# A one-layer encoder kernel: tile offsets of 512 bytes, and another order of its first loads

## The chip, the core and the metric

The kernel runs on one core of a Trainium2 chip. The core has a matrix engine, TensorE (PE; its weight loads are shown apart, as PEld), three engines for elementwise work, VectorE (DVE), ScalarE (ACT) and GpSimd (POOL), and SyncE (SP), which here issues most of the DMAs. A tile lies in SBUF, 128 partitions of one and the same byte offset each; matmul results go to PSUM, in banks of 128x512 floats. The metric is the device time of one execution in microseconds (us), the median of several runs.

## What is computed

One residual layer on x of 1024 tokens by 1024 channels, in float32: a norm; one projection into pooling channels and q, k, v; a pooling mixer; differential attention with 8 heads; two gated branches; an output projection; then a norm and a squared-ReLU MLP of width 4096. Cut to what matters:

```python
h = rmsnorm(x, g_mix[l])
z = h @ w_in[l]
...
y_pool = pool_mixer(u_pool, w_pool_grp[l], pool_scale[l])
y_attn = diff_attention(q, k, v, g_q[l], g_k[l], lam, g_sub[l], lambda_init)
gates = jax.nn.sigmoid(h @ w_gate[l] + b_gate[l])
merged = (gates[..., :D_MODEL] * (y_pool @ w_branch_pool[l])
          + gates[..., D_MODEL:] * (y_attn @ w_branch_attn[l]))
x = x + merged @ w_out[l]
h2 = rmsnorm(x, g_ffn[l])
x = x + jnp.square(jax.nn.relu(h2 @ w_up[l])) @ w_down[l]
```

The rmsnorm is `x * rsqrt(mean(x*x) + EPS) * g`, with g a row of 1024 numbers that every token uses.

## The kernel before

**Products.** Every float32 operand is split in two parts of a reduced format, hi and lo (`split`, L117: a cast on ACT, then a subtraction on DVE or POOL, L119 and L120). A product is three matmuls, hi by hi, hi by lo, lo by hi (`mm3`, L125 to L127). In `nc.tensor.matmul(ps, a, b)` a is the weights (128x128, loaded anew for every matmul) and b the columns that stream past them (128x512 for most groups, 128x384 for z, 128x256 for po).

**Stages.** In order of time: norm and projection z per head and token tile, with attention (scores sc, transposed maps ta, output po) interleaved, and in the gaps the gate projection g and the pooling projection u; then bp (pool branch), ba (attention branch), op (output projection), and the MLP. The MLP multiplies by a scheme of seven block products instead of eight: X, Y, Z, W for the up projection (16 pairs), and Da, Db for the down projection (56 steps of 24 matmuls). A planner orders the instructions of each engine by priority and dependence; `issue_after` holds back a block of instructions on one engine until a given one of that engine has been issued.

**Places in SBUF.** Tiles are taken from pools, and pools lie one behind the other in the order in which they are opened: const (identf, mhalf, ones, inv, cols, gs, zero, and two buffers each of nss and nrs), hp0 and hp1 (hT, later mT and others), wpool (split weights: wqkv, fwgate, wba, wo), rpool, fp (fr, and two buffers of fo, 528 floats each), fq, up (U tiles: K, V, maps, yT, raw inputs), and, during attention, sp, which holds small tiles (ss, rs, rows, ms, nm, cf) and larger ones (dist, qn, Q, oqs) mixed. Each tile takes a multiple of 32 bytes per partition. The MLP's pools replace these; some grow from the left again (BT tiles, A and AS operands, and w in the last stage), those with side="right" from the top of SBUF downwards (B11 and B21, the raw weights, and u in the last stage).

**The start.** START (L43) lists the first steps. `x0` loads the first token tile in two halves (L322); `g` loads the row g into all 128 partitions of gmb (L368); `n0` norms token tile 0 (`norm_transpose`, halves=True: one half's sum of squares on ACT at L268, the other's on DVE at L269, the power on POOL at L274), multiplies x by rs and g (L280), transposes on TensorE (L285) and splits into hT; `w0` to `w3` load the weights of the first head, two issues each (L332); `s` steps split them. All these loads go through SP's queue, in that order. Then follow the small loads rows, gqk and lqk (L373 to L381). The first z product needs hT of tile 0 and the split weights.

```python
START = "x0 g n0 w0 w1 w2u w3u x1 s0p s1 x2 s2p s3 x3"
...
gmb = ut([P, D], F32, "gmb")
nc.sync.dma_start(gmb, g_mix[0].partition_broadcast(P))
...
nc.vector.scalar_tensor_tensor(hn[:, js], xt[:, js], rs, gb[:, js], op0=ALU.mult, op1=ALU.mult)
```

Of the kernel before, what the change touches and what calls it, by code (L numbers as in the profile page):

```python
# [17 lines left out]
P = 128  # L18
S = 1024
# [22 lines left out]

START = "x0 g n0 w0 w1 w2u w3u x1 s0p s1 x2 s2p s3 x3"  # L43
NX = [-2, -1, 0, 0, 0, 1, 2, 3]
# [13 lines left out]
def encoder_kernel(  # L58
# [26 lines left out]

    const = ctx.enter_context(tc.tile_pool(name="const", bufs=1))
    dram = ctx.enter_context(tc.tile_pool(name="dram", bufs=1, space=DRAM))
    mix = ctx.enter_context(ExitStack())
# [25 lines left out]
    def f(ap):  # L114
        return ap.bitcast(F32)
# [25 lines left out]
    def fo_tile(name):  # L141
        return fp.tile([P, 528], F32, tag="fo", name=name, bufs=N_FO)

# [92 lines left out]

    identf = const.tile([P, P], F32, name="identf")
    make_identity(nc, identf)
    mhalf = const.tile([P, NT], F32, name="mhalf")
    nc.gpsimd.memset(mhalf, -0.5)  # L240
    ones = const.tile([P, P], F32R, name="ones")
    nc.gpsimd.memset(f(ones), 1.0)
# [3 lines left out]

    cols = const.tile([P, 32], F32, name="cols")
    gs = const.tile([P, 1], F32, name="gs")
# [12 lines left out]
    def norm_transpose(xt, gb, t, dst, hn, small, banks, halves=False):  # L261
# [16 lines left out]
        for j in range(2):  # L278
            js = slice(j * 512, (j + 1) * 512)
            nc.vector.scalar_tensor_tensor(hn[:, js], xt[:, js], rs, gb[:, js], op0=ALU.mult, op1=ALU.mult)  # L280
            trp, trtag = banks[j % len(banks)]
            ps = trp.tile([P, 512], F32, tag=trtag, name=f"hps{t}_{j}")
            for i in range(4):
                k = 4 * j + i
                nc.tensor.transpose(ps[:, i * P : (i + 1) * P], hn[:, k * P : (k + 1) * P], identf)  # L285
# [12 lines left out]

    with ExitStack() as ph:
        sp = ph.enter_context(tc.tile_pool(name="sp", bufs=1))  # L300
        ps_s = ph.enter_context(tc.tile_pool(name="ps_s", bufs=N_S, space=PSUM))
# [3 lines left out]
        def s1(shape, dt, name, tag, bufs=1):  # L305
            return sp.tile(shape, dt, tag=tag, name=name, bufs=bufs)

        xs = {}

# [8 lines left out]
        def load_x(t):  # L318
            xs[t] = ut([P, D], F32, f"x{t}")
            for c in range(0, D, 512 if t == 0 else D):  # L320
                e = c + 512 if t == 0 else D
                nc.sync.dma_start(xs[t][:, c:e], x[t * P : (t + 1) * P, c:e])  # L322

# [4 lines left out]

        def load_w(h, kp, raw_fn=raw):
            rw = raw_fn([P, 2, 384], f"rqkv{h}_{kp}")  # L330
            for i in range(2):
                nc.sync.dma_start(  # L332
                    rw[:, i, :].rearrange("p (s c) -> p s c", s=3),
                    w_qkv[:, 2 * kp + i, :, h * P : (h + 1) * P],
                )
            raws[h, kp] = rw

        def norm_x(t):
            if t % 4 == 0:
                hT.update(alloc_T(htile, "hT", t // 4))  # L340
            if FU >> t & 1:
                hn = fu_tile(f"hn{t}")
            else:
                hn = ut([P, D], F32, f"hn{t}")
            banks = [(ps_t, "tr"), (ps_s, "sc")][: 2 if t < N_SC else 1]
            norm_transpose(xs.pop(t), gmb, t, hT, hn, sp, banks, t == 0)

# [9 lines left out]
        for w in START.split():  # L357
            if w[0] == "x":
                load_x(int(w[1]))
            elif w[0] == "n":  # L360
                norm_x(int(w[1]))
            elif w[0] == "w":
                load_w(0, int(w[1]), utf if w[2:] else raw)
            elif w[0] == "s":
                split_w(0, int(w[1]), nc.gpsimd if w[2:] else nc.vector)
            elif w[0] == "g":
                gmb = ut([P, D], F32, "gmb")
                nc.sync.dma_start(gmb, g_mix[0].partition_broadcast(P))  # L368


        rows = sp.tile([32, P], F32, name="rows")
        nc.gpsimd.memset(rows, 0.0)
        nc.sync.dma_start(rows[0:16, :], b_gate[0].rearrange("(r p) -> r p", p=P))  # L373
# [18 lines left out]
        def columns():  # L392
            cols_ps = ps_t.tile([P, 512], F32, tag="tr", name="cols_ps")
            nc.tensor.transpose(cols_ps[:, 0:32], rows, identf[0:32, 0:32])
            nc.vector.tensor_copy(cols, cols_ps[:, 0:32])
            nc.vector.tensor_scalar(gs, cols[:, 20:21], 1.0 - LAMBDA_INIT, None, op0=ALU.mult)
# [66 lines left out]
        def stage_qkT(h, t):  # L463
# [302 lines left out]
    gate_units = gates()  # L766
    for _ in range(G_FIRST):
        next(gate_units)
# [563 lines left out]
```

## Time and profile before

| | |
|---|---|
| median of 3 runs | 1557.21 us (1557.16 to 1557.71) |
| the profiled execution | 1556.93 us, its span 1555.1 us |
| first matmul | 8.89 us after the span's start |
| matmuls | 7649, of which 553 are transposes |
| stages by start of their matmuls | z from 10.9, bp 702.4 to 746, ba 746.0 to 836, op 836 to 928, MLP up 929 to 1243, MLP down from 1243.5 |
| mean DMA rate | 133 GB/s |

The profile is one execution, taken on the chip. A row of the timeline gives start and duration in us, the engine, the line, the operation, the tiles (written <- read) and, in brackets, how long the engine had been idle and what ended that. A group's row gives the same for all instructions of a kind, with their count and either the busy time and the mean ns of one, or minimum, median and maximum in ns. A window's row gives, for a stretch of the span, the busy time of an engine and its count of instructions, then the granted clock, the share of the DMA engines and GB/s. Ends of matmuls are modelled, so a matmul of 0.39 us can be followed by another 0.23 us after its start; what counts is the distance from start to start.

### The profile page before, as it was taken

The numbers are of one execution on the slowest core, as the hardware profiler recorded it, in microseconds if no ns is written. First come the engines' busy times: TensorE is split into PE (matmuls) and PEld (weight loads), VectorE is DVE, ScalarE is ACT, GpSimd is POOL, SyncE is SP. The second block draws the span as 40 slices with busy tenths as digits, with TensorE's granted clock in tenths as the row PEclk, the third lists the DMA queues.
The fourth block names the chain that finished last, engine by engine and source line by source line (L and its number), as shares of the span: only waits on it lengthen the run. The fifth ranks groups of instructions, "written<-read, shape, count | busy, mean of one in ns | idle before, by whom it ended". The sixth has DMA issues, their size and how long they took to land.

```text
span 1555.1 us, 22054 instructions
## 1 busy us (share of the span) xinstructions
PE 1535.1 (99%) x7649; PEld 1321.5 (85%) x7649; DVE 1012.4 (65%) x2268; ACT 816.0 (52%) x1808; POOL 350.2 (23%) x447
## 2 busy tenths in 40 slices
PE   7999999999999999999999999999999999999999
PEld 6999999999998989888888887888888788888887
DVE  6777677777878787765322448766665668556662
ACT  6656556656566556566432456565555634333331
POOL 5433334243425262324453400000000000000000
PEclk9999999999999999999999999999999999999999
DMA  7111212021202031547426524554432789537750
GB/s 229 47 56 48 65 41 68 24 74 40 72 28 84 28 96 42 176 151 235 143 92 198 178 102 122 179 183 159 136 135 109 273 312 385 179 122 256 224 189 27
DMA packets 166681, 206.41 MB, mean 133 GB/s; under 512 B 10069, under 2 KB 102954, under 8 KB 166570
## 3 DMA queue, kind: packets, MB, share of 16 engines
q1 hardware_dynamic: 149162, 177.71, 35.3%
q10 hardware_dynamic: 17408, 27.30, 4.7%
q8 instruction: 60, 0.98, 0.3%
q14 instruction: 51, 0.42, 0.1%
HBM read 150.42 MB, written 54.56 MB: 132 GB/s over the span
## 4 chain that ended last, share of the span: by engine, by line
PE 89%; DVE 4%; issue 2%; DMA 2%; ACT 2%; POOL 1%; POOLq 0%; SPq 0%; ACTq 0%; DVEq 0%
PE z L125 5%; PE z L127 5%; PE z L126 5%; PE Da L126 4%; PE Da L125 4%; PE Da L127 4%; PE g L125 3%; PE g L126 3%; PE g L127 3%; PE Db L126 3%; PE Db L125 3%; PE Db L127 3%; PE X L125 2%; PE X L126 2%; PE X L127 2%; PE sc L509 2%
## 5 line engine op out<-in xcount | busy, mean ns | idle before, releaser
L125 PE MATMUL z<-wqkv,hT 128*128 128x384 f32 x512 | 174.9, 342 | 0.5 <-DVE qn L451 0.3
L127 PE MATMUL z<-wqkv,hT 128*128 128x384 f32 x512 | 174.7, 341 | 0.5 <-DVE hT L120 0.4
L126 PE MATMUL z<-wqkv,hT 128*128 128x384 f32 x512 | 174.0, 340 | 0.0
L520 ACT ACTIVATE s<-s,nm 128x256 f32<-128x256 f32 (+7 forms) x128 | 99.6, 778 | 45.4 <-DVE nm L512 40.7
L259 POOL TENSOR_TENSOR ms<-ms,mhalf 128x4 f32<-128x4 f32 x64 | 66.5, 1040 | 159.0 <-DVE ms L258 140.6
L126 PE MATMUL g<-hT,fwgate 128*128 128x512 f32 x256 | 101.1, 395 | 0.0
L125 PE MATMUL g<-hT,fwgate 128*128 128x512 f32 x256 | 101.0, 394 | 0.1
L127 PE MATMUL g<-hT,fwgate 128*128 128x512 f32 x256 | 101.0, 395 | 0.0
L125 PEld LDWEIGHTS z<-wqkv,hT 128*128 128x128 f32 x512 | 97.1, 190 | 4.3 <-DVE qn L451 1.0
L127 PEld LDWEIGHTS z<-wqkv,hT 128*128 128x128 f32 x512 | 96.9, 189 | 3.1 <-DVE hT L120 1.2
L126 PEld LDWEIGHTS z<-wqkv,hT 128*128 128x128 f32 x512 | 97.1, 190 | 2.9
L512 DVE CUSTOM_DVE_ANT_0 s<-sc,dist 128x512 f32<-128x512 f32 (+3 forms) x128 | 74.6, 586 | 19.5 <-PE sc L510 18.1
L120 POOL TENSOR_TENSOR wqkv<-rqkv,wqkv 128x384 fp32r<-128x384 f32 x60 | 63.7, 1078 | 19.8 <-ACT wqkv L119 19.8
L120 DVE TENSOR_TENSOR AS<-s,AS 128x512 fp32r<-128x512 f32 x64 | 43.9, 688 | 36.1 <-ACT AS L119 35.9
L509 PE MATMUL sc<-K,Q 128*128 128x512 f32 (+2 forms) x192 | 66.8, 354 | 0.1
L510 PE MATMUL sc<-K,Q 128*128 128x512 f32 (+2 forms) x192 | 66.4, 354 | 0.0
L457 POOL TENSOR_TENSOR qn<-qn,ggh 128x128 f32<-128x128 f32 x64 | 32.3, 505 | 138.7 <-DVE qn L451 127.6
L483 ACT CAST Q<-tk 64x128 fp32r<-64x128 f32 x128 | 33.2, 259 | 57.9 <-DVE Q L482 56.0
L480 ACT CAST Q<-tk 64x128 fp32r<-64x128 f32 x128 | 33.0, 258 | 53.5 <-DVE K L479 52.1
L120 POOL TENSOR_TENSOR fwgate<-frgate,fwgate 128x512 fp32r<-128x512 f32 x32 | 43.9, 1376 | 52.3 <-ACT fwgate L119 52.1
L127 PEld LDWEIGHTS g<-hT,fwgate 128*128 128x128 f32 x256 | 48.1, 188 | 8.7
L125 PEld LDWEIGHTS g<-hT,fwgate 128*128 128x128 f32 x256 | 48.2, 188 | 7.4 <-ACT go L755 0.4
(429 smaller groups left out, 4647.0 us busy)
## 6 DMA issues: line engine op xcount, KB each, us to landing
wd<-in_w_down_dram SPq DMA_DIRECT2D x56, 512.0 KB, 5.3
wu<-in_w_up_dram SPq DMA_DIRECT2D x32, 512.0 KB, 5.0
udS<-us SPq DMA_DIRECT2D x64, 256.0 KB, 2.2
ur<-udS SPq DMA_DIRECT2D x32, 512.0 KB, 3.5
rqkv<-in_w_in_dram SPq DMA_DIRECT2D x64, 192.0 KB, 2.8
ud<-u ACTq DMA_DIRECT2D x48, 256.0 KB, 2.9
ur<-ud SPq DMA_DIRECT2D x24, 512.0 KB, 4.9
frgate<-in_w_gate_dram SPq DMA_DIRECT2D x32, 256.0 KB, 2.8
```

The source lines that it names most:

```text
L120: (lo_eng or nc.vector).tensor_tensor(lo, src, f(hi), op=ALU.subtract)
L125: nc.tensor.matmul(ps, lhs_hi, rhs_hi, start=first, stop=False, **kw)
L126: nc.tensor.matmul(ps, lhs_hi, rhs_lo, start=False, stop=False, **kw)
L127: nc.tensor.matmul(ps, lhs_lo, rhs_hi, start=False, stop=last, **kw)
L259: nc.gpsimd.tensor_tensor(dst, dst, mhalf[:, :n], op=ALU.pow)
L457: nc.gpsimd.tensor_tensor(qn[:, 2:4, :], qn[:, 2:4, :], ggh.unsqueeze(1).broadcast_to([P, 2, HD]), op=ALU.mult)
L480: nc.scalar.copy(q_hi, q)
L483: nc.scalar.copy(Q[other, m, 1, :], q)
L509: nc.tensor.matmul(dst, Q[:, i, 0, :], rhs, start=True, stop=False)
L510: nc.tensor.matmul(dst, Q[:, i, 1, :], rhs, start=False, stop=True)
L512: nc.vector.tensor_tensor_reduce(out=s[i][:, c : c + w], in0=sc[:, 0:w], in1=dist[:, o0 + c : o0 + c + w], scale=2.0 ** -(h + 1), scalar=B ...
L520: nc.scalar.activation(s[i][:, 0:n], s[i][:, 0:n], AF.Exp, bias=last, scale=-1.0, accum_out=Z[:, i, t : t + 1])
```

## The change

- Two pools are new: units, behind const, for identf and ones, and sq, ahead of sp, for the larger attention tiles (dist, Q, and those made by `s1`). cols is cut to its 24 used columns, a fo tile gets 576 floats instead of 528, and a tile edge of 120 floats is put at the top of the right side.
- The row g is loaded as one row, on ACT's queue, and spread over the partitions by two matmuls of a row of ones with it, into two PSUM banks. The first norm reads g there; then g is copied from there to gmb for the other norms.
- The order of START: w1 is loaded on ACT's queue (the letter a), ahead of n0; x1 comes before w3, and x2 after the third split. n0 is put behind the last DMA issue on ACT.
- The small loads and the first unit of gate work are put behind the last load of a token tile of START on SP's queue.

```diff
-START = "x0 g n0 w0 w1 w2u w3u x1 s0p s1 x2 s2p s3 x3"
+START = "x0 g w1ua n0 w0 w2 x1 w3u s0p s1 s2p x2 s3 x3"
...
     const = ctx.enter_context(tc.tile_pool(name="const", bufs=1))
+    units = ctx.enter_context(tc.tile_pool(name="units", bufs=1))
...
-        return fp.tile([P, 528], F32, tag="fo", name=name, bufs=N_FO)
+        return fp.tile([P, 576], F32, tag="fo", name=name, bufs=N_FO)
...
-    identf = const.tile([P, P], F32, name="identf")
+    identf = units.tile([P, P], F32, name="identf")
...
-    ones = const.tile([P, P], F32R, name="ones")
+    ones = units.tile([P, P], F32R, name="ones")
...
-    cols = const.tile([P, 32], F32, name="cols")
+    cols = const.tile([P, 24], F32, name="cols")
...
-            nc.vector.scalar_tensor_tensor(hn[:, js], xt[:, js], rs, gb[:, js], op0=ALU.mult, op1=ALU.mult)
+            nc.vector.scalar_tensor_tensor(hn[:, js], xt[:, js], rs, gb[j], op0=ALU.mult, op1=ALU.mult)
...
     with ExitStack() as ph:
+        sq_pool = ph.enter_context(tc.tile_pool(name="sq", bufs=1))
         sp = ph.enter_context(tc.tile_pool(name="sp", bufs=1))
...
         def s1(shape, dt, name, tag, bufs=1):
-            return sp.tile(shape, dt, tag=tag, name=name, bufs=bufs)
-
-        xs = {}
+            return sq_pool.tile(shape, dt, tag=tag, name=name, bufs=bufs)
+
+        xs, issued = {}, {}
...
-                nc.sync.dma_start(xs[t][:, c:e], x[t * P : (t + 1) * P, c:e])
+                issued[nc.sync] = nc.sync.dma_start(xs[t][:, c:e], x[t * P : (t + 1) * P, c:e]).ins
...
-        def load_w(h, kp, raw_fn=raw):
+        def load_w(h, kp, raw_fn=raw, queue=nc.sync):
...
-                nc.sync.dma_start(
+                issued[queue] = queue.dma_start(
...
-            norm_transpose(xs.pop(t), gmb, t, hT, hn, sp, banks, t == 0)
+            gb = g_ps if t == 0 else [gmb[:, 0:512], gmb[:, 512:D]]
+            norm_transpose(xs.pop(t), gb, t, hT, hn, sp, banks, t == 0)
+            if t == 0:
+                for j in range(2):
+                    nc.vector.tensor_copy(gmb[:, j * 512 : (j + 1) * 512], g_ps[j])
...
-                norm_x(int(w[1]))
+                with tc.issue_after(issued[nc.scalar]):
+                    norm_x(int(w[1]))
             elif w[0] == "w":
-                load_w(0, int(w[1]), utf if w[2:] else raw)
+                load_w(0, int(w[1]), utf if "u" in w else raw, nc.scalar if "a" in w else nc.sync)
...
-                nc.sync.dma_start(gmb, g_mix[0].partition_broadcast(P))
+                g_row = ut([1, D], F32, "g_row")
+                nc.scalar.dma_start(g_row, g_mix)
+                g_ps = [pool.tile([P, 512], F32, tag=tag, name=f"g_ps{tag}") for pool, tag in ((ps_o, "o"), (ps_f, "f"))]
+                for j, ps in enumerate(g_ps):
+                    nc.tensor.matmul(ps, f(ones)[0:1, :], g_row[:, j * 512 : (j + 1) * 512], start=True, stop=True)
...
         rows = sp.tile([32, P], F32, name="rows")
+        late = ExitStack()
+        started = issued[nc.sync]
+        late.enter_context(tc.issue_after(started))
...
-
-        dist = sp.tile([P, S], F32, name="dist")
+        late.close()
+
+        dist = s1([P, S], F32, "dist", "dist")
...
-            Q = sp.tile([P, 2, 2, P], F32R, tag="Q", name=f"Q{h}_{t}", bufs=N_Q)
+            Q = s1([P, 2, 2, P], F32R, f"Q{h}_{t}", "Q", N_Q)
...
-    for _ in range(G_FIRST):
+    with tc.issue_after(started):
+        next(gate_units)
+    for _ in range(G_FIRST - 1):
         next(gate_units)
...
+    edge = ctx.enter_context(tc.tile_pool(name="edge", bufs=1, side="right"))
+    nc.gpsimd.memset(edge.tile([P, 120], F32, name="edge"), 0.0)
     nb_pool = pool_of(hs, "nb", 4, side="right")
```

More of the change, by code (lines that the diff above doesn't have):

```diff
@@ L327, in encoder_kernel @@
         raws = {}
-        def load_w(h, kp, raw_fn=raw):
+        def load_w(h, kp, raw_fn=raw, queue=nc.sync):
             rw = raw_fn([P, 2, 384], f"rqkv{h}_{kp}")
             for i in range(2):
-                nc.sync.dma_start(
+                issued[queue] = queue.dma_start(
                     rw[:, i, :].rearrange("p (s c) -> p s c", s=3),
                     w_qkv[:, 2 * kp + i, :, h * P : (h + 1) * P],
-                )
+                ).ins
             raws[h, kp] = rw
@@ L394, in columns @@
             nc.tensor.transpose(cols_ps[:, 0:32], rows, identf[0:32, 0:32])
-            nc.vector.tensor_copy(cols, cols_ps[:, 0:32])
+            nc.vector.tensor_copy(cols, cols_ps[:, 0:24])
             nc.vector.tensor_scalar(gs, cols[:, 20:21], 1.0 - LAMBDA_INIT, None, op0=ALU.mult)
```

## The prediction

> **What bounds the kernel now.** I read the page first: busy times, the slices, the chain.
>
> ```profile
> span 1555.1 us, 22054 instructions
> PE 1535.1 (99%) x7649; PEld 1321.5 (85%) x7649; DVE 1012.4 (65%) x2268; ACT 816.0 (52%) x1808; POOL 350.2 (23%) x447
> PE   7999999999999999999999999999999999999999
> PE 89%; DVE 4%; issue 2%; DMA 2%; ACT 2%; POOL 1%; POOLq 0%; SPq 0%; ACTq 0%; DVEq 0%
> ```
>
> TensorE sets the time. Only the first slice, 39 us, has idle PE. So a gain comes from a quicker start or from matmuls that follow one another faster. For the second I asked for the PE instructions of single tiles (ns min/median/max), then for windows in which only one group runs, and for the scores in the view that keeps shapes apart (busy us, mean ns).
>
> ```profile
> L126 PE MATMUL bp<-ypT,wbp x64: 389/389/395, 702.6 to 745.6; 128*128 128x512 f32 x64
> L126 PE MATMUL X<-BT2l,AS x64: 388/389/398, 956.7 to 1230.3; 128*128 128x512 f32 x64
> L126 PE MATMUL ba<-yT,wba x128: 387/395/398, 746.3 to 835.1; 128*128 128x512 f32 x128
> L126 PE MATMUL X<-B11l,A x64: 391/394/477, 929.3 to 1211.2; 128*128 128x512 f32 x64
> L126 PE MATMUL Y<-B21l,A x64: 393/394/398, 929.8 to 1214.0; 128*128 128x512 f32 x64
> L125 PE MATMUL Da<-w_0h,u_0h x32: 392/392/392, 1243.5 to 1512.0; 128*128 128x512 f32 x32
> L126 PE MATMUL Da<-w_0l,u_0h x32: 394/394/394, 1243.7 to 1512.2; 128*128 128x512 f32 x32
> L127 PE MATMUL Da<-w_0h,u_0l x32: 388/388/388, 1244.0 to 1512.4; 128*128 128x512 f32 x32
> L126 PE MATMUL u<-hT,fwpool x64: 387/393/398, 286.5 to 574.8; 128*128 128x512 f32 x64
> L126 PE MATMUL g<-hT,fwgate x256: 387/393/496, 31.3 to 701.9; 128*128 128x512 f32 x128
> L126 PE MATMUL z<-wqkv,hT x512: 331/334/522, 11.4 to 626.9; 128*128 128x384 f32 x171
> L126 PE MATMUL po<-AT_0l,V x96: 274/283/365, 87.5 to 690.7; 128*128 128x256 f32 x96
> L510 PE MATMUL sc<-K,Q 128*128 128x512 f32 x96 | 37.9, 395 | 0.0
> ...
> 712.00:745.00 33.00, 33.00 (x147) 1.00 0.58 173
> 747.00:835.00 88.00, 88.00 (x379) 1.00 0.34 108
> 1245.00:1505.00 260.00, 260.00 (x1138) 1.00 0.70 241
> ```
>
> One shape, 128x512, has medians from 388 to 395 ns. The windows show that the difference is paid on the clock: 33 us over 147 matmuls is 0.2245 to 0.227 us from start to start (one or two are cut at the edges), 88 over 379 is 0.232 to 0.233, 260 over 1138 is 0.2285. So bp's 389, ba's 395 and D's 391.3 (mean of its three rows) stand for about 227, 233 and 228.5 ns.
>
> What separates the groups is where their tiles lie. Counting the tile sizes in the order of the pools, each rounded up to 32 bytes, behind the four constants of L1318: 128 + 512 (identf) + 32 + 512 (ones) + 64 + 128 (cols) + 2x32 + 4x32 = 1568, which is 32 past a multiple of 512. All tiles of the pools hp0, hp1, wpool start there, and the left pools of the MLP. Two fo tiles of 2112 bytes move what follows (up, fq) to 160; small tiles in sp move Q to 416; right-hand pools grow down from a top 32 bytes below a multiple of 512, so their tiles lie at 480. Hence bp and BT2 have both operands at 32; ba reads weights at 32 and columns at 160; X, Y from B11 and B21 32 and 480; D 480 and 32; sc 416 and 160. **Equal offsets have the 389, unequal ones the 391 to 395.** The exception is g and u: equal, but mixed in time with sc and po.
>
> **The change: alignment.** The constants now come to 128+32+64+96+6x32 = 512, fo to 2304 bytes (two are 9x512), small tiles go to sp behind sq, and edge (120x4 = 480 bytes) brings the right side to a multiple. So every large operand is at 0, all offsets equal. Cost against 389 ns: ba 384x6 = 2.3 us; the B11 and B21 products 384x5 = 1.9; D 1344x2.3 = 3.1; sc 192x(395-389) = 1.1, by L510's mean, in which waits stand too; g and u 960x4 = 3.8. That is 12.2 us. For z and po the median stands 3 and 9 ns above the minimum: at most 1536x3 + 544x9 = 9.5 us more. I take ba, B, D and sc in full (8.4), half of g and u (1.9), as the cause there is only inferred, and 0.7 of z and po, near nothing because z already has equal offsets: **11 us**, between 0 and 21.7.
>
> Whether offset 0 is as good as an equal 32 no row shows, since nothing lies at 0; this sets the outer bounds below. Here the Trainium skill speaks against the change. "TensorE: Matmul & The Clock Gate", Part 2, says that PE reads the moving operand and the weights through two independent ports, so that loading the next weights takes nothing from the running matmul, and "SBUF — State Buffer", section "Who interferes with whom", that PE never waits on anyone. By that, offsets are worth nothing (rival C). The trace disagrees: one shape, 389 against 395.
>
> **The change: the start.** Timeline of the first 18 us (start, duration), then the chain that ended last (start, duration), and rows that serve for prices.
>
> ```profile
> 0.73 1.28 ACT L268 ACT_TABLE_LOAD   x1 [0.73 <-PEq L1318]
> 0.91 0.20 POOL L242 MEMSET ones<- 128x128 f32 x1
> 1.65 0.42 SPq L368 DMA_DIRECT2D gmb<-in_g_mix_dram  x1
> 3.34 0.63 ACT L268 ACTIVATE hn<-x 128x512 f32<-128x512 f32 x1 [1.32 <-DMA x<-in_x_dram]
> 3.87 0.19 ACT L268 ACTIVATION_READ_ACCUMULATOR hn<-x 128x1 f32 x1
> 4.39 0.69 DVE L269 CUSTOM_DVE_ANT_0 hn<-x 128x512 f32<-128x512 f32 x1 [4.39 <-DMA x<-in_x_dram]
> 5.58 0.56 POOL L274 TENSOR_TENSOR rs<-rs,mhalf 128x1 f32<-128x1 f32 x1 [3.45 <-DVE rs L273]
> 8.08 1.42 DVE L280 SCALAR_TENSOR_TENSOR hn<-x,rs,gmb 128x512 f32<-128x512 f32 x2 [2.66 <-DMA gmb<-in_g_mix_dram]
> 8.71 0.51 ACT L119 CAST wqkv<-rqkv 128x384 fp32r<-128x384 f32 x1 [4.65 <-DMA rqkv<-in_w_in_dram]
> 8.89 1.97 PE L285 MATMUL hps<-identf,hn 128*128 128x128 f32 x8 [8.89 <-DVE hn L280]
> 10.91 0.69 PE L125 MATMUL z<-wqkv,hT 128*128 128x384 f32 x1
> ...
> 16.33 0.32 PE z L127
> 16.65 0.22 PE z L125
> ...
> 17.05 0.17 PE z L127
> 17.91 0.17 PE z L126
> ...
> 943.47 0.68 DVE L120 TENSOR_TENSOR A<-wu,A 128x512 fp32r<-128x512 f32 x1
> 44.24 0.34 ACTq L756 DMA_DIRECT2D g_dram<-go  x1
> L332 SPq DMA_DIRECT2D rqkv<-in_w_in_dram x12: 381/488/2404, 2.1 to 19.2; - x12
> 6.00:12.00 6.00, 2.98 (x10) 2.07 (x10) 2.79 (x5) 2.79 (x7) 2.15 (x3) 1.00 1.15 311
> 12.00:18.00 6.00, 5.88 (x22) 5.88 (x23) 4.49 (x10) 4.30 (x10) 3.30 (x3) 1.00 0.85 299
> ```
>
> What ends last before the first matmul is gmb: rs is ready at 5.58+0.56 = 6.14, but L280 starts at 8.08, when the copy of g in 128 partitions has landed. The change sends one row of 4 KB instead and spreads it by two matmuls. That wait goes: 8.08-6.14 = **1.9 us**. Late next are rs itself and the weights. These came at 8.71 and later because gmb's 512 KB stood ahead of them on SP's queue, in a stretch where the DMA share is 1.15. Without it, and with w1 issued from ACT, the splits can start while the norm is still computed, so z's first matmuls wait less.
>
> The upper bound: the first 24 z matmuls take 10.91 to 18.08, 7.2 us; at 0.17 (the rows after 17.05) they would take 4.1. The 0.32 rows up to 16.33 show a slow stretch of PE, at a granted clock that reads 1.00. The two new matmuls would let PE begin work earlier, and so may end that stretch earlier: 0 to 3.1 us. I take 1.1, nearer to nothing, because the splits and the landing of x1 still pace this stretch. Start: 1.9+1.1 = **3 us**, between 0 and 5.
>
> Against it stand: three DMA issues ahead of the table load and L268 on ACT, 0.34+2x0.49 = 1.3 us. ACT then has its half square at 0.73+1.3+1.28+0.63+0.19 = 4.1, one us before DVE's half ends (4.39+0.69 = 5.08), so it is hidden; at the longest issue of the row, 2.4 us, it would cost up to 1. w1 on a second queue shares the DMA engines with x0's second half: up to one half-transfer, 4.39-3.34 = 1.05 us, later; that is in the lower bound. Two copies of g into gmb, 0.68 each: DVE is busy 2.79 and 4.49 of 6 us, so they fit; if not, 1.4 us. The two matmuls with one row of weights have no row; PE is idle until 8.89, so up to 5 us of them is hidden. The small loads (rows, gqk, lqk) go behind x3 on SP's queue, and the first gate weights with them: as gmb (0.42) and w1 (two issues of 0.49) leave that queue, what is ahead of them goes out sooner; late, they would hold up gg (L399) and so the first qn, not the z matmuls. Edge's memset is one of 0.2 us on POOL, busy 23%. These cost nothing.
>
> **Sum.** 11+3 = 14 us off 1555.1 of span (1556.93 for that execution, 0.3 below the median of 1557.21): about **1543**.
>
> **Rivals.** A, the forecast: 1557.2-14 = 1543, with its bounds 1531 to 1557. Chance 0.66.
>
> B, offset 0 is better than an equal 32. For: z's matmuls stand 0.32 apart in the slow stretch and 0.172 after ((17.91-17.05)/5), not 0.16, so some 12 ns of each fast one aren't array time. If a start inside a 512-byte block caused all of that, 7096 matmuls that aren't transposes would save 85 us: 1469; for half, 1512. Against: the 12 ns are there with all offsets, and may belong to every change of weights. The skill's TensorE page, Part 1, gives 2.5 ns over the array time for matmuls back to back, which would be near the full case. Chance 0.13.
>
> C, offsets are worth nothing and what I read is some other trait of the groups: only the start gains, 1557.2-3 = 1554. For: g and u. Against: D's three rows, which repeat to the nanosecond. Chance 0.13.
>
> D, slower: at equal offset 0, weights and columns meet at every block border, and all 4824 matmuls of 512 columns run like ba. Place: L125 to L127; price 4824x6-12.2 = 16.7 us, less the start: 1571. It decides from a mean of 389+(12.2+3)/4.82 = 392 ns on. Against: equal 32 and equal 32 do not collide. Chance 0.08.
>
> **Numbers.** Two in a thousand, 3 us, is what a measurement here can tell from no change. Faster: A 0.65, B 0.13, half of C 0.06. Same: A 0.01, the rest of C. Slower: D. The range takes in A from 1531 up, C and the mild end of B: 1525 to 1557, some 8 in 10.
>
> **What would show it.** Right: medians of ba, of X and Y from B11 and B21 and of all three D rows at 388 to 389, windows of 227 ns; L280 starting near 6.2 and z before 9.5. B would show as 512-column medians well under 387. C: the medians stay, D's three rows keep their 388 to 394. D: 392 or more in bp and BT2. Wrong at the start: L268 or x0's second half later than 4.4, or L280 waiting for PE. A new idle stretch over 2 us on PE anywhere else would fall outside all of this.

## The result, and the profile after

The changed kernel takes 1549.4 us (median of 6 runs, 1547.97 to 1550.2), the kernel before 1557.43 beside it (6 runs, 1557.16 to 1558.01): a ratio of 0.9947, with a 95% interval from 0.9934 to 0.996. It is 8.0 us faster; 14 were forecast. The profiled execution has a span of 1548.4 us against 1555.1, so 6.7 us are to be found in the two traces. The page of the changed kernel, its span, PE's slices and the shares of the chain:

```profile
span 1548.4 us, 22069 instructions
PE   8999999999999999999999998999999999999999
PE 92%; DVE 3%; issue 2%; ACT 1%; POOL 1%; DMA 1%; POOLq 0%; SPq 0%; ACTq 0%; DVEq 0%
```

TensorE still sets the time. The digit 8 in slice 25 is new: a wait near 958 us, to which we come back. The first slice has 8 instead of 7, but the two products of g, 4 us that weren't there before, are in it. Next the PE instructions of single tiles (ns min/median/max, first and last start) and the scores in the view that keeps shapes apart (busy us, mean ns). Lines L125 to L127 of before are L126 to L128 now.

```profile
L127 PE MATMUL bp<-ypT,wbp x64: 387/389/393, 702.5 to 745.5; 128*128 128x512 f32 x64
L127 PE MATMUL ba<-yT,wba x128: 389/389/389, 746.2 to 832.6; 128*128 128x512 f32 x128
L127 PE MATMUL X<-B11l,A x64: 389/389/473, 926.7 to 1207.4; 128*128 128x512 f32 x64
L127 PE MATMUL Y<-B21l,A x64: 389/389/402, 927.2 to 1210.1; 128*128 128x512 f32 x64
L126 PE MATMUL Da<-w_0h,u_0h x32: 389/389/389, 1239.8 to 1505.7; 128*128 128x512 f32 x32
L128 PE MATMUL Da<-w_0h,u_0l x32: 389/389/389, 1240.2 to 1506.1; 128*128 128x512 f32 x32
L126 PE MATMUL g<-hT,fwgate x256: 387/391/497, 27.5 to 701.6; 128*128 128x512 f32 x128
L127 PE MATMUL z<-wqkv,hT x512: 331/334/522, 10.0 to 626.9; 128*128 128x384 f32 x171
```

```profile
L525 PE MATMUL sc<-K,Q 128*128 128x512 f32 x96 | 38.0, 396 | 0.0
```

The windows of ba and of the down projection (us, PE busy and its count, then the other engines, the granted clock, the DMA share, GB/s):

```profile
747.00:832.00 85.00, 85.00 (x377) 70.41 (x376) 23.60 (x33) 30.21 (x46) 43.63 (x34) 1.00 0.33 108
1245.00:1505.00 260.00, 260.00 (x1149) 215.35 (x1148) 168.74 (x158) 96.56 (x96) 0.00 (x0) 1.00 0.70 245
```

The reader is to see two things. First, ba, the B11 and B21 products and D (the third of its rows, not shown, too) stand at 389 now, the best value of before, and the windows confirm it on the clock: 85 us hold 377 products of ba (0.2255 us each; 0.232 before), 260 us hold 1149 of D instead of 1138. Second, g, z and the scores sc are where they were: the mean of g is 395 ns before and after, that of z 340 to 342, that of sc's second line 395 and 396.

Where the 6.7 us come from can be read from the starts of the stages. bp begins at 702.5 (702.6 before), so **in these two executions the first 700 us bring 0.1 us**. One execution says little here: in five kernels below that have the same start, bp begins between 700.2 and 701.7. From bp to the start of the up projection, stages with equal offsets repeat to within 0.1 us. ba is 2.4 us shorter (88.8 us from 746.3 to 835.1 before, 86.4 from 746.2 to 832.6 now). D's 1344 products take 1344x(0.2285-0.2263) = 3.0 us less. The up projection, from X to Da, is only 1.1 us shorter (314.2 us from 929.3 to 1243.5 before, 313.1 from 926.7 to 1239.8 now), although its 384 products from B11 and B21 are faster: 389 ns instead of 394 in the rows, and from start to start 227 instead of 233 (the mean distance of neighbours in the two traces), which is worth 384x6.2 = 2.4 us. What eats it is in the view of PE's waits from 935 to 965 us (total us, times, longest), of the changed kernel, a row of DVE in its timeline, and the same waits of the kernel before:

```profile
PE X L126 <- ACT AS L120: 2.1, 1, 2.1
PE Z L126 <- ACT BT1h L120: 1.5, 1, 1.5
PE Y L126 <- DVE u L878: 0.8, 1, 0.8
```

```profile
955.49 0.69 DVE L881 TENSOR_TENSOR y<-y 128x512 f32<-128x512 f32 x1 [2.46 <-DMA y<-nd]
```

```profile
PE Z L125 <- ACT BT1h L119: 1.4, 1, 1.4
PE Y L125 <- DVE u L861: 0.8, 1, 0.8
PE W L125 <- ACT A L119: 0.7, 1, 0.7
```

4.4 us of waits against 2.9. DVE stands 2.46 us for a block of nd (1.9 before), and the operands S come 0.6 us later, counted from X's first product. That alone would have cost nothing. Before, twelve products of W and six of Y stood between X's products from BT2 and those from BT3, and PE came to the latter 35.7 us after X's first product. Now they come next, at 31.6 us, and X waits 2.1 us for the operand AS.

The start, in the changed kernel (start, duration, and in brackets the idle time before it and what ended it):

```profile
4.93 0.69 DVE L270 CUSTOM_DVE_ANT_0 hn<-x 128x512 f32<-128x512 f32 x1 [4.93 <-DMA x<-in_x_dram]
6.71 0.75 DVE L281 SCALAR_TENSOR_TENSOR hn<-x,rs,g_pso 128x512 f32<-128x512 f32 x1 [0.75 <-POOL rs L275]
7.38 0.68 DVE L352 COPY gmb<-g_pso 128x512 f32<-128x512 f32 x1
8.64 0.68 DVE L352 COPY gmb<-g_psf 128x512 f32<-128x512 f32 x1
8.84 2.27 POOL L121 TENSOR_TENSOR wqkv<-rqkv,wqkv 128x384 fp32r<-128x384 f32 x2 [0.23 <-ACT wqkv L120]
9.24 2.29 DVE L121 TENSOR_TENSOR wqkv<-rqkv,wqkv 128x384 fp32r<-128x384 f32 x2
9.54 0.67 PE L126 MATMUL z<-wqkv,hT 128*128 128x384 f32 x1
11.45 0.41 DVE L121 TENSOR_TENSOR hT<-hps,hT 128x256 fp32r<-128x256 f32 x1
11.92 0.69 PE L128 MATMUL z<-wqkv,hT 128*128 128x384 f32 x1 [1.38 <-DVE rs L259]
12.17 0.54 DVE L121 TENSOR_TENSOR wqkv<-rqkv,wqkv 128x384 fp32r<-128x384 f32 x1
17.31 0.52 PE L127 MATMUL z<-wqkv,hT 128*128 128x384 f32 x1
```

The wait for gmb is gone: L281 follows rs. z begins at 9.54 instead of 10.91. But the third product needs the low part of hT, and DVE makes that only after two subtractions of wqkv that take 2.29 us, beside POOL's two (alone, at 12.17, one takes 0.54), and after the two copies of g into gmb, 0.68 each; DVE has no pause from 6.71 on. So PE, done with the second product at about 10.5, stands until 11.92. (The view names rs, the shorter DVE instruction behind; the operand is hT.) And z's rows are still 0.32 us apart at 17.31, against 16.33 before.

### The profile page after: what moved, and what is told of

Read it like the earlier page. It is cut to its first block, busy times and chain, and to the rows that moved or that the text cites. A ratio compares the mean times of both kernels' runs of the same rounds, so it can differ in the third digit from the quotient of the medians.

```text
span 1548.4 us, 22069 instructions
## 1 busy us (share of the span) xinstructions
PE 1530.6 (99%) x7653; PEld 1323.4 (85%) x7653; DVE 1014.7 (66%) x2270; ACT 816.1 (53%) x1808; POOL 351.2 (23%) x448
## 4 chain that ended last, share of the span: by engine, by line
PE 92%; DVE 3%; issue 2%; ACT 1%; POOL 1%; DMA 1%; POOLq 0%; SPq 0%; ACTq 0%; DVEq 0%
PE z L126 5%; PE z L128 5%; PE z L127 5%; PE Da L127 4%; PE Da L128 4%; PE Da L126 4%; PE g L126 4%; PE g L128 4%; PE g L127 4%; PE Db L127 3%; PE Db L126 3%; PE Db L128 3%; PE X L126 2%; PE X L128 2%; PE X L127 2%; PE sc L524 2%
## 5 line engine op out<-in xcount | busy, mean ns | idle before, releaser
L128 PE MATMUL z<-wqkv,hT 128*128 128x384 f32 x512 | 174.6, 341 | 1.4 <-DVE rs L259 1.4
L126 PE MATMUL z<-wqkv,hT 128*128 128x384 f32 x512 | 174.7, 342 | 0.8 <-ACT hT L120 0.5
L127 PE MATMUL z<-wqkv,hT 128*128 128x384 f32 x512 | 174.1, 340 | 0.0
L126 PE MATMUL g<-hT,fwgate 128*128 128x512 f32 x256 | 101.0, 395 | 0.1
L128 PE MATMUL g<-hT,fwgate 128*128 128x512 f32 x256 | 101.0, 395 | 0.0
L127 PE MATMUL g<-hT,fwgate 128*128 128x512 f32 x256 | 101.0, 395 | 0.0
L126 PEld LDWEIGHTS z<-wqkv,hT 128*128 128x128 f32 x512 | 97.1, 190 | 4.2 <-DVE qn L466 1.0
L128 PEld LDWEIGHTS z<-wqkv,hT 128*128 128x128 f32 x512 | 96.9, 189 | 3.5 <-DVE rs L259 1.9
L127 PEld LDWEIGHTS z<-wqkv,hT 128*128 128x128 f32 x512 | 96.9, 189 | 3.0
L128 PEld LDWEIGHTS g<-hT,fwgate 128*128 128x128 f32 x256 | 48.1, 188 | 8.7
L126 PEld LDWEIGHTS g<-hT,fwgate 128*128 128x128 f32 x256 | 48.2, 188 | 7.3 <-ACT go L770 0.4
```

The lines of the kernel that those rows point to most:

```text
L126: nc.tensor.matmul(ps, lhs_hi, rhs_hi, start=first, stop=False, **kw)
L127: nc.tensor.matmul(ps, lhs_hi, rhs_lo, start=False, stop=False, **kw)
L128: nc.tensor.matmul(ps, lhs_lo, rhs_hi, start=False, stop=last, **kw)
```

## The experiments: tiles and start apart

Two kernels take one half of the change each. The first keeps the new places of the tiles and has the old start.

```diff
-START = "x0 g w1ua n0 w0 w2 x1 w3u s0p s1 s2p x2 s3 x3"
+START = "x0 g n0 w0 w1 w2u w3u x1 s0p s1 x2 s2p s3 x3"
...
-                g_row = ut([1, D], F32, "g_row")
-                nc.scalar.dma_start(g_row, g_mix)
...
+                nc.sync.dma_start(gmb, g_mix[0].partition_broadcast(P))
```

> The tiles lie as in the changed kernel (all large ones at 0), the start is that of before. Theory 'spacing': ba, X, Y, Da and Db have medians of 389 ns in all rows, which took 2.5+2.7+3.0 = 8.2 us out of the matmuls; the new idle of PE in the up projection, some 1.5 us, is back too: 6 to 8 us faster than before, about 1550. Theory 'start': the start brought 3 us of the 8, so this one gains 5 or less: 1552 and more. bp starts at 702 under 'spacing', at 705 under 'start'.

Measured: 1549.1 us (1547.76 to 1549.49), ratio 0.9947 [0.9935, 0.996]. That is the whole gain.

The second has the new start and the old places (fo of 528, no edge, one pool for small and large tiles):

```diff
-        return fp.tile([P, 576], F32, tag="fo", name=name, bufs=N_FO)
+        return fp.tile([P, 528], F32, tag="fo", name=name, bufs=N_FO)
...
-    nc.gpsimd.memset(edge.tile([P, 120], F32, name="edge"), 0.0)
```

> The start of the changed kernel, the tiles where they were before. Theory 'spacing': the first matmul of z comes 1.4 us earlier, but the lead is lost by 20 us; bp starts at 702 as before, Da keeps 392, 394, 388: 1557, within 1 us of before. Theory 'start': bp starts at 699 and the time is 1554.

Measured: 1557.02 us (1554.86 to 1559.91), ratio 1.0001 [0.9992, 1.001]. The start by itself brings nothing that can be measured, and its executions spread over 5 us. Its trace has the late S too (PE stands 2.0 us from 958.0 on), the first kernel's hasn't: the stall in the up projection came with the start, 940 us earlier. No step of the start touches these tiles. What links them is the planner, for in the traces both PE and DVE have another order in the up projection with the new start: PE as told above, and on DVE one addition `u<-Y,x` now goes ahead of the operands S. That this order makes the stall is read from the traces; no run has changed it alone.

## The experiments: which offsets cost

All of these are the changed kernel with other sizes of edge (which moves the right-hand tiles), of fo (which moves what lies in up, so the columns of ba) and of cols (which moves everything on the left). The first puts every large tile at 32, left and right:

```diff
-    cols = const.tile([P, 24], F32, name="cols")
+    cols = const.tile([P, 32], F32, name="cols")
...
-    nc.gpsimd.memset(edge.tile([P, 120], F32, name="edge"), 0.0)
+    nc.gpsimd.memset(edge.tile([P, 112], F32, name="edge"), 0.0)
```

> The changed kernel with all large tiles at 32 past a multiple of 512 instead of at 0, left and right. Theory 'difference': only the distance of the two operands' offsets counts; ba, B11, B21, Da, Db all at 389 and the time is that of the changed kernel, 1549. Theory 'zero': a tile has to start at a multiple (of 512, or of 64); then bp, BT and D stand at other values than 389 where they were 389 in the changed kernel, or ba and D go back to 392 to 395, some 6 us slower: 1555.

Measured: 1548.07 us (1547.85 to 1548.72), ratio 0.9942 [0.9929, 0.9956]; ba, B and D at 389 as in the changed kernel. Offset 0 is nothing special; the title's "offsets of 512 bytes" are one way to get equal offsets.

The next four leave the left at 0 and shift the other side.

```diff
-        return fp.tile([P, 576], F32, tag="fo", name=name, bufs=N_FO)
+        return fp.tile([P, 584], F32, tag="fo", name=name, bufs=N_FO)
...
-    nc.gpsimd.memset(edge.tile([P, 120], F32, name="edge"), 0.0)
+    nc.gpsimd.memset(edge.tile([P, 56], F32, name="edge"), 0.0)
```

> The changed kernel with the right-hand pools 256 bytes and the pools from up on 64 bytes off; so ba has weights at 0 and columns at 64, D weights at 256 and columns at 0, B11 and B21 weights at 0 and columns at 256. Theory 'difference': all three leave 389, as with 128 and 448 before: ba 391 to 395, D's rows apart by up to 6 ns, B 391 to 395; about 6 us slower than the changed kernel. Theory 'line': only offsets that aren't multiples of 64 bytes cost, and all stay at 389.

One execution, 1550.66 us. PE's rows of ba (columns at 64) and D (weights at 256):

```profile
L126 PE MATMUL ba<-yT,wba x128: 393/395/398, 744.3 to 831.5; 128*128 128x512 f32 x128
L127 PE MATMUL ba<-yT,wba x128: 387/389/397, 744.5 to 831.7; 128*128 128x512 f32 x128
L128 PE MATMUL ba<-yT,wba x128: 391/392/394, 744.8 to 832.0; 128*128 128x512 f32 x128
...
L126 PE MATMUL Da<-w_0h,u_0h x32: 388/390/390, 1240.3 to 1506.1; 128*128 128x512 f32 x32
```

(bp, with both operands at 0, has 390 in this execution too.) A distance of 256 costs nothing: from 1250 to 1510 us D has 1148 products, in the changed kernel 1149. This also says why sc had nothing to give: its operands lay at 416 and 160 before, 256 apart. The three rows of ba, 395, 389 and 392, look like those of D before (392, 394, 388): there the weights lay 64 below the columns, counted modulo 512, as here.

Now the right side lies at 128 and the columns of ba at 256 (edge of 88, fo of 608):

> The changed kernel with edge of 88 floats and fo of 608: the right-hand tiles (u, B11, B21) lie at offset 128, the columns of ba at 256, all else at 0. Theory 'distance': what costs is the difference of the offsets of weights and columns, taken to the nearest multiple of 256; 256 is free, 64 costs some 2.3 ns a matmul, 128 some 6.6 (as ba before, 160 against 32). Then ba stays at 389 to 390 in all three rows, D's and B's rows rise to a mean near 395, and the stages D and B take 1728x6.6 = 11.4 us more than in the changed kernel: some 1561 us. Rival 'group': every group has a price of its own and any difference that isn't a multiple of 256 brings it; then D and B stand at 391 to 394 as in the kernel before, some 1555 us.

The right side at 64 and the columns of ba at 384 (edge of 104, fo of 624):

> The changed kernel with edge of 104 floats and fo of 624: right-hand tiles at 64, the columns of ba at 384. Theory 'distance': 384 is 128 from a multiple of 256, so ba has a mean near 395 again (some 2.5 us more), and D and B have their three rows apart with means near 391 (some 5.7 us more): 1557 to 1558 us, as the kernel before. Rival 'sign': columns that lie 128 below a multiple of 512 aren't like columns that lie 128 above one, and ba stays at 389. Rival 'group' (above): the same numbers as 'distance' here, so it is the run before this one that tells these two apart.

and 32 for the right side alone (edge of 112):

> The changed kernel with edge of 112 floats alone: right-hand tiles at 32, all else at 0. Theory 'distance', by a straight line from 0 at 0 to 2.3 ns at 64: D and B near 390.2, 1728x1.2 = 2 us more than the changed kernel, 1551.5 us. Rival 'block': only differences of 64 bytes and more cost; medians stay at 389, 1549.4 us. Rival 'group': 391 to 394, 1555 us.

Measured: 1559.04, 1562.95 and 1561.87 us, one execution each. Their rows of ba and D, in this order (behind the second's a window of its down projection; for the last, D and Y):

```profile
L127 PE MATMUL ba<-yT,wba x128: 389/389/389, 745.6 to 831.9; 128*128 128x512 f32 x128
...
L126 PE MATMUL Da<-w_0h,u_0h x32: 390/393/404, 1241.0 to 1513.6; 128*128 128x512 f32 x32
```

```profile
L127 PE MATMUL ba<-yT,wba x128: 387/395/398, 744.8 to 833.7; 128*128 128x512 f32 x128
L126 PE MATMUL Da<-w_0h,u_0h x32: 393/396/398, 1243.6 to 1517.3; 128*128 128x512 f32 x32
```

```profile
1250.00:1510.00 260.00, 260.00 (x1116) 209.50 (x1115) 161.61 (x149) 93.59 (x94) 0.00 (x0) 1.00 0.69 236
```

```profile
L126 PE MATMUL Da<-w_0h,u_0h x32: 392/395/396, 1242.5 to 1516.2; 128*128 128x512 f32 x32
...
L126 PE MATMUL Y<-B21h,A x64: 393/396/780, 925.9 to 1212.6; 128*128 128x512 f32 x64
```

That window holds 1116 products where the changed kernel has 1149 in as long: 0.233 against 0.2263 us. So all three theories fall in part. "Group" falls with D, which has 388 to 394, 392 to 393 or 396 as its offset says. "Distance" is right for 256 (free) and for 384 (as 128), but a small distance isn't a small cost: weights 32 or 64 above the columns make D as dear as ba was before, some 6.7 ns a product, 1344x(0.233-0.2263) = 9 us. "Block" falls with 32. Collected, weights' offset minus columns' offset, modulo 512, the medians of the rows, and the mean distance in ns from start to start of neighbouring products of the group, worked out from the traces:

| difference | group and kernel | medians | start to start |
|---|---|---|---|
| 0 | ba, B, D of the changed kernel | 389 | 227 |
| 256 | ba (columns at 256); D (weights at 256) | 389; 390 | 227; 227 |
| 32 | D, right side at 32 | 395 to 396 | 233 |
| 64 | D, right side at 64; B11 and B21 products before | 396; 394 | 233; 233 |
| 128 | D, right side at 128; ba, columns at 384 | 392 to 393; 394 to 395 | 232; 233 |
| 384 (128 below) | ba before; B11 and B21 products, right side at 128 | 394 to 395; 392 to 394 | 233; 233 |
| 448 (64 below) | D before; ba, columns at 64; B11 and B21 products, right side at 64 | 388 to 394; 389 to 395; 388 to 394 | 229; 229; 230 to 231 |
| 480 (32 below) | B11 and B21 products, right side at 32 | 394 to 396 | 233 to 234 |

The last column is simpler than the medians. 0 and 256 are free, weights 64 below the columns cost 2 to 4 ns, and every other difference that was tried costs 6 to 7. So the sign counts (64 above is dear, 64 below cheap), and a median can hide a part of the price: with the right side at 128 D's row reads 390/393/404, and its window holds 1120 products, 0.232 us each.

What in the memory does this isn't settled; the runs show the differences and their prices, no more. The two rules of the Trainium skill that the prediction weighed, the two independent ports ("TensorE: Matmul & The Clock Gate", Part 2) and a PE that never waits ("SBUF — State Buffer", "Who interferes with whom"), give one price for all of these rows; the runs don't agree, with 389 to 396 ns for one shape by nothing but the place of the tiles. Nor is the offset all: g and sc, with equal offsets in the changed kernel, stay at 395 and 396 in the mean, and no run says why.

## The experiments: where the start's lead went

In the first of these one letter moves the two subtractions that stood ahead of hT from DVE to POOL:

```diff
-START = "x0 g w1ua n0 w0 w2 x1 w3u s0p s1 s2p x2 s3 x3"
+START = "x0 g w1ua n0 w0 w2 x1 w3u s0p s1p s2p x2 s3 x3"
```

> The changed kernel with one letter more in START: the two subtractions of s1 go to POOL instead of DVE. In the changed kernel z begins 1.4 us earlier than before but then PE waits 1.4 us, from 10.5 to 11.9, for the low part of hT, which stands on DVE behind these two subtractions (9.24 to 11.53). Theory 'order': this wait took the lead away; with the two gone from DVE it shrinks below 0.5 us, the work done by 20 us rises by about 1 us, and the median falls to some 1548.4. Theory 'slow stretch': PE runs z at half speed until a point that differs from execution to execution (14.3 to 17.8 us in the runs so far), so a us won inside it is worth half of one or less; the wait shrinks, but the median stays within 0.7 us of 1549.4. Theory 'POOL': POOL, which now has six subtractions of some 1 us each from 6.6 us on, gives s2's part later than z needs it, and PE waits there instead: 1549.4 or more.

Measured: 1558.74 us (1556.64 to 1560.35), ratio 1.0009 [1.0, 1.0018]: all of the gain is lost. PE's second and third product of z, the longest of its waits from 9 to 60 us, and bp:

```profile
10.28 0.52 PE L127 MATMUL z<-wqkv,hT 128*128 128x384 f32 x1
10.60 0.52 PE L128 MATMUL z<-wqkv,hT 128*128 128x384 f32 x1
```

```profile
PE hps L286 <- DVE hT L121: 3.1, 2, 2.2
```

```profile
L127 PE MATMUL bp<-ypT,wbp x64: 388/389/397, 711.2 to 754.2; 128*128 128x512 f32 x64
```

The local part of theory "order" is right: the third product follows at 10.60 without a wait. Theory "POOL" has the sign but not the place, since z's first 24 products run without a wait for s2. None foresaw what came of the edit: bp's row begins at 711.2, 8.7 us later than in the changed kernel. PE's order in the trace is another all through the attention: the planner took one letter at 7 us as a reason to plan it anew, and the new plan has other waits, such as 2.2 us of PE for a low part of hT, and 6.7 us in all from 400 to 660 us where the changed kernel has 1.2. The stall near 958 us, though, is gone, and PE has the order of the kernel before there.

The second goes back to the old START and keeps g by TensorE:

```diff
-START = "x0 g w1ua n0 w0 w2 x1 w3u s0p s1 s2p x2 s3 x3"
+START = "x0 g n0 w0 w1 w2u w3u x1 s0p s1 x2 s2p s3 x3"
...
-                nc.scalar.dma_start(g_row, g_mix)
+                issued[nc.scalar] = nc.scalar.dma_start(g_row, g_mix).ins
```

> The changed kernel, g spread by PE from one row, but START in the order of the kernel before and all weights on SP's queue. 46 PE instructions stand elsewhere than in the changed kernel. Theory 'g is all': x0's second half lands near 4.4 instead of 4.9, rs is ready near 6.1, and the wait for gmb is gone all the same, so that z's first product comes at 9.0 to 9.5 as in the changed kernel. Theory 'second queue': without w1 on ACT's queue the splits come later, and PE waits for them after z's first products as it did for the low part of hT: z's first 24 products end no earlier than in the changed kernel. In both the median is 1548 to 1550: what is won at the start is the 1.4 us of the first product, and a part of it falls into the slow stretch. A median above 1551 would say that the place of the instructions in the planner's order outweighs all this.

Measured: 1551.92 us (1549.39 to 1552.28), ratio 0.9961 [0.995, 0.9973], 2.5 us slower than the changed kernel and 2.8 slower than the kernel with the new places and the whole old start. x0's second half comes at 4.95 here too, so w1 on ACT's queue isn't needed to make it late; "g is all" falls on that and on z, which begins at 10.53, behind subtractions of wqkv on DVE; "second queue" falls as well, for z's first 24 products are done by 17.4 us, when the changed kernel still has slow rows. Yet bp begins 1.8 us later than in the changed kernel (704.1 against 702.3), with new waits of PE behind 20 us (1.4 and 1.2 us for parts of hT): as the expectation said of a median above 1551, the planner's order outweighs both. The stall for AS is here too, 2.0 us, with the old START; so the new order of the loads isn't needed for it.

The other three try to end z's slow stretch earlier. The prediction had hoped that PE's work on g would do it. Two kernels put products of ones by ones (128x128) ahead of g's, 14 and 26 of them, into a bank that g's product overwrites:

```diff
+                for i in range(26):
+                    nc.tensor.matmul(g_ps[0][:, 0:P], ones, ones, start=True, stop=True)
                 for j, ps in enumerate(g_ps):
```

> The changed kernel with 14 products of ones by ones (128x128, fp32r, into a bank that g's product overwrites) ahead of the two products of g, so that PE works from about 1.2 us on instead of 2.3. Of all PE instructions 25 stand elsewhere than in the changed kernel, all in the first 45 us or so; on DVE some of the up projection stand elsewhere too, where the changed kernel has its stall of 2.3 us (957.7). Theory 'slow stretch': PE runs at half speed until it has worked for some us without a pause, whatever it works on; the stretch then ends earlier than the 13.2 to 17.8 us of the runs so far in most executions, and the median falls by 0.5 to 1.5 us; with the later stall back at 0.9, 1.4 more: 1546.5 to 1548.9. Rival 'data': the first 15 us are paced by splits and hT alone; then only the later stall can bring something: 1548 to 1549.4. Rival 'pause': the idle PE between 6.0 and 7.5 us sets the count back; as 'data'.

> The same with 26 products, some 2.8 us at half speed, so that PE works from about 1.2 us until the transposes; 34 PE instructions stand elsewhere than in the changed kernel, all early, and nothing after that, so the later stall of 2.3 us stays. Theory 'slow stretch': some 13 z products take 0.17 instead of 0.32 us each, up to 2 us less, and executions spread less: 1547.4 to 1549. Rival 'data': as the changed kernel, 1549.4. Rival 'late g': the products of g begin at about 4 instead of 2.3 us and end at 7.7, at half speed, so that rs waits for g (6.7 in the changed kernel) and z begins up to 1 us later: 1549.4 to 1550.4.

Measured: 1551.46 us (1549.65 to 1553.41), ratio 0.9961 [0.9949, 0.9973], and 1557.05 (1555.91 to 1561.27), ratio 1.0002 [0.9993, 1.0012]: slower than the changed kernel by 2.1 and 7.7. In the first, z is slow until 17.7 us and the later stall is 2.0 us, so "slow stretch" falls, and 1551.46 lies above what any of its theories gave. PE of the second:

```profile
1.17 5.81 PE L379 MATMUL g_pso<-ones 128*128 128x128 f32 x26 [1.17 <-POOL ones L243]
6.91 2.07 PE L381 MATMUL g_pso<-g_row,ones 1*128 1x512 f32 x2
...
19.54 0.52 PE L127 MATMUL z<-wqkv,hT 128*128 128x384 f32 x1
```

The 26 products took 0.22 us each, not the 0.11 that the expectation had counted with, so g came 4.6 us late (rival "late g", with a larger price), and z is as slow as ever at 19.54, after 18 us in which PE was mostly busy. bp begins 5.6 us later than in the changed kernel (707.9); the rest of this trace's loss is in the up projection, where the granted clock is 0.50 from 965.7 to 968.7 us. The last kernel has 12 products of 512 columns instead, the same 128 read four times:

```diff
+                wide = ones.rearrange("p (a b) -> p a b", a=1).to_broadcast([P, 4, P])
+                for i in range(12):
+                    nc.tensor.matmul(g_ps[0], ones, wide, start=True, stop=True)
```

> The changed kernel with 12 products of ones by four times the same 128 columns (128x512, fp32r) ahead of the two products of g: at half speed some 5.1 us of PE work of the width that z's products have, from 1.2 to 6.3 us, against the 5.8 us of 128x128 products in the run with 26, after which z was as slow as ever, until 19.9 us. Eight PE instructions stand elsewhere than in the changed kernel, all early. Theory 'wide work': PE's half speed ends when it has worked for one whole stretch of some 3.4 us on products that keep the array itself busy, counted by a clock of its own; small products with their weight loads don't keep it busy enough. Then in many executions the stretch ends ahead of z: z's rows are 0.17 apart from the first on, the products of g take half of their 3.7 us, and the time is 1548 to 1550 in such executions, in spite of g's later start; in the others as 'late'. Rival 'late': work ahead of the first real products doesn't count; g's products end near 10 us, z begins near 11.5 and stays slow for 3 to 6 us: 1551 to 1553.

Measured: 1550.48 us (1548.49 to 1550.83), ratio 0.9954 [0.9941, 0.9968]. PE in the timeline, then windows of PE alone behind the products of g, and one of z's slow rows (the granted clock is the third number from the end):

```profile
1.17 4.35 PE L380 MATMUL g_pso<-ones 128*128 128x512 f32 x12 [1.17 <-POOL ones L243]
5.46 1.12 PE L382 MATMUL g_pso<-g_row,ones 1*128 1x512 f32 x2
9.94 0.69 PE L126 MATMUL z<-wqkv,hT 128*128 128x384 f32 x1 [1.21 <-ACT hT L120]
...
17.22 0.52 PE L128 MATMUL z<-wqkv,hT 128*128 128x384 f32 x1
```

```profile
6.50:7.40 0.90, 0.90 (x3) 1.00 1.17 353
7.50:8.60 1.10, 0.98 (x4) 0.50 1.08 425
...
12.40:17.50 5.10, 5.10 (x19) 4.79 (x19) 4.70 (x15) 3.75 (x9) 2.10 (x4) 0.50 0.72 256
```

Here wide work does end the slow stretch: the first half of g takes 1.12 us instead of 2.07. But the clock is down again, at 0.50, from 7.5 us on, and stays there in z until 17.5. PE's pauses, from 8.7 to 9.9 and from 10.9 to 11.5 us, for hT and for the second half of hn, come later than that: until 7.4 PE had worked without one, at the end on the products of g, whose weights are one row. What closes the clock isn't shown. So "wide work" is right about what opens the clock and wrong about the gain. No kernel of the study is shown to beat the changed one; the one with all tiles at 32 has an interval that overlaps its own.

## Why the prediction was right, and where its sizes were off

**The forecast and the range.** Rival A, faster by equal offsets, came true, and 1549.4 lies in the range of 1525 to 1557. The point, 1543, was 6.4 us too low. The range alone proves little, for C's 1554 lies in it too; what tells A from C is the two kernels with half of the change each.

**Alignment: 11 forecast, about 8 measured.** Three of the terms taken in full were right: ba 2.3 (2.4 in the trace), D 3.1 (3.0), and B, 1.9 by its medians and 2.4 by the distance of its starts. Together they measure 7.8, and the kernel with the places alone gains 7.9 us (1557.02 to 1549.1). Wrong were the terms that went by a group's mean or median without a difference of offsets that was known to cost: sc 1.1, half of g and u 1.9, z and po 0.7. They came to nothing: sc's mean is 396 now and g's 395 as before; u's medians fell from 392 or 393 to 389, but its means are 392 to 393 in both traces. For sc the reason is shown (416 and 160 are 256 apart, and 256 is free); g, u, z and po had equal offsets before.

**"Equal offsets have the 389, unequal ones the 391 to 395"** held for ba, B and D, but as a rule was too coarse: 256 apart is as good as equal, the price depends on the sign and reaches 396, and g, the prediction's own exception, has equal offsets and medians of 390 to 393 still.

**The start: 3 forecast, 0 measured**, by the interval of the start alone between 1.2 us gained and 1.6 lost. The 1.9 us of the wait for gmb did go, less 0.5 for the second half of x0. The step that failed is "the splits can start while the norm is still computed, so z's first matmuls wait less": they did start earlier, and thereby got ahead of the low part of hT on DVE, which costs PE 1.4 us. The two copies of g, for which the prediction saw room on DVE at no cost, stand in the same queue and take 1.4 us of it; moving the splits alone ended the wait, moving the copies wasn't tried. And "the two new matmuls would let PE begin work earlier, and so may end that stretch earlier" is refuted: products of g and even 26 small ones ahead of z don't end it. Under "wrong at the start" the prediction had named x0's second half later than 4.4: it came at 4.93.

**The stall outside all this.** "A new idle stretch over 2 us on PE anywhere else" came, near 958 us, 2.1 us long. PE's waits there grew by 1.5 us in all in the profiled execution. The prediction had weighed each moved step on its own queue, but not that the planner, given another start, writes another order 900 us later.

**The rivals.** B, offset 0 better than 32, falls with 1548.07 for all tiles at 32. C, offsets worth nothing, falls with the places alone. D, equal offsets that collide, falls with 389 in ba, B and D.

## What to carry to other kernels

Where every product loads its weights anew, as here, its two operands are best laid at the same offset modulo 256 bytes; groups of one shape whose rows differ by a few ns are worth a look at their tiles' addresses, and at the distance from start to start, since the price is paid where TensorE is busy throughout. Under a planner that orders all instructions, a gain of 1 us at the start isn't a gain until the stages behind it have been read again: one moved step lost 9 us here. Judge such an edit by the start of the next large stage over several executions, not by its own neighbourhood.

## What the runs showed of the hardware

- The place of the tiles alone moves a 128x512 product from 389 to 396 ns (0.2263 to 0.233 us from start to start). Equal offsets and offsets 256 bytes apart cost the same.
- z's 0.32 us per 384 columns at the start is PE at half clock, although the profile reads 1.00 there: in the last kernel, where the clock had been opened once and fell back, the same 0.32 stands beside a granted clock of 0.50. So the 1.00 before the first recorded change can't be trusted; the spacing of equal products can.
- The clock opens after wide products without a pause (within the 4.35 us of 12 such products), and not after 5.8 us of 128x128 ones, in one trace each; it closed again at 7.5 us although PE had not paused. "TensorE: Matmul & The Clock Gate" of the Trainium skill, Part 1, describes a gate that opens after one busy window of about 3.4 us, counted by a window that runs freely, so that the same kernel varies; the traces agree in that z's slow stretch ended anywhere from 13.2 to 19.9 us.
- The same happens in the middle: after PE had waited 1.5 and 0.8 us near 943 to 946 us, some executions run seven products or so at half clock, as in these two rows and this window of the kernel with the places alone, 7x(0.427-0.227) = 1.4 us. Six of the fourteen traces have such a stretch in the up projection, among them the kernels with the right side at 32 and at 64; that of the changed kernel hasn't.

```profile
947.05 0.63 PE L127 MATMUL Y<-B21l,A 128*128 128x512 f32 x1
947.48 0.63 PE L128 MATMUL Y<-B21h,A 128*128 128x512 f32 x1
```

```profile
946.20:949.00 2.80, 2.80 (x8) 2.24 (x7) 2.80 (x5) 2.80 (x7) 0.00 (x0) 0.50 0.00 0
```

- A subtraction of 128x384 on DVE takes 0.54 us alone and 1.14 beside POOL's (2.29 for two). "SBUF — State Buffer", section "Who interferes with whom", says that an operation of DVE with both inputs in SBUF contends with POOL's reads; the trace agrees.
